# A two-layer diffusion trunk on one core: operand buffers 96 bytes further on, smaller steps between sub-layers, and one modulation unit moved

## The chip, the core and the metric

The kernel runs on one core of a Trainium2 chip. The metric is the time of one execution in microseconds on the device. The core's engines are TensorE (PE in the profile, with PEld for its weight loads), VectorE (DVE), ScalarE (ACT), GpSimd (POOL) and SyncE (SP), which here issues the loads of the weights. Each engine works through a list of instructions in order, and waits where an instruction needs the result or the buffer of another engine.

## The reference

The reference is a small model of two layers over 384 tokens of width 1024: 128 context tokens and 256 latent ones. Each layer has three sub-layers, a SwiGLU feed-forward (hidden width 2816), a token mixer (attention and convolution in layer 0, pooling and grouped-query attention in layer 1), and a second feed-forward. All is computed in 32-bit floating point. Each sub-layer normalises, scales and shifts its input, and gates its normalised output:

```python
def modulate_norm(x, g, shift, scale):
    return rms_norm(x, g) * (1.0 + scale[:, None, :]) + shift[:, None, :]

def swiglu(h, w1, w2):
    g, u = jnp.split(h @ w1, 2, axis=-1)
    return (jax.nn.silu(g) * u) @ w2
```

Shift, scale and gate come from SiLU of a conditioning vector through a linear map of its own for each layer, nine vectors of 1024 per layer and per kind of token.

## The kernel before

The tokens lie in three tiles of 128 (tile 0 is the context, tiles 1 and 2 are latent). The six sub-layers are numbered 0 to 5: feed-forward, even mixer, feed-forward, feed-forward, odd mixer, feed-forward. A product in full precision is made of three float32r products: an operand is split in a high part (a cast on ScalarE) and a low part (a subtraction on VectorE), and `mm3` (lines 436 to 438) multiplies high by high, high by low and low by high. The activations of all tiles lie in `xh` and `xl`, columns by token.

**Weights.** They come as units of 1 MB. SP loads a unit to one of four `raw` buffers. A unit is used in two halves: `prep` casts a half to `whi` on ScalarE (line 152) and subtracts on VectorE to get `wlo` (line 155), into one of three pairs of buffers. With `defer`, the subtraction is cut in two pieces of 512 columns that are issued later. A list of units, made once by `plan()`, sets the order of the loads. The linear map of the modulation is in the list too, as units called `mod`: VectorE computes each of these in four pieces (line 229, tile `junkv`), which the kernel sets between the subtractions of the weights. `MOD_PLAN` has a pair of numbers for each sub-layer: how many modulation units stand among its weights, and how many of these in its first phase (the 22 units of the gate and up weights, `w1`). The rest stand in its second phase (the 11 units of the down weights, `w2`), spread over its first seven places.

**Second phase.** `down` multiplies the hidden activations `g` by the down weights and gathers into two PSUM banks per tile, 512 columns each. Its main part is 15 halves over all three tiles; the last halves are then done tile by tile, so that a tile's sum is ready early and can be worked on beside the others' matmuls.

**Between sub-layers.** For each tile, `post_steps` squares the sums with a running total (ScalarE, line 329, tile `junk`), multiplies them by the gate (VectorE, line 353, `ptmp`), computes one over the root of the mean square in `rstd_of` (ScalarE's square root `rq`, VectorE's `rv`, `ry`, `ra`, `rz`), and adds to the residual `x` (line 365). `stat_steps` squares the new `x`, and scales it to `xn`, one half on VectorE (line 382) and one on ScalarE (line 383). TensorE transposes `xn` into two PSUM banks (line 389), and `evac_steps` applies scale and shift from the bank into `xtmp` (line 411 on VectorE for the first two of four blocks of 128 columns, line 413 on ScalarE for the other two), and splits `xtmp` into `xh` (line 422) and `xl` (line 423). For tile 2 this runs beside the next sub-layer's first matmuls: `early(0)` to `early(3)` work on tiles 0 and 1 with a half of the weights each, and the transposes of tile 2 are issued by `between` inside `early(2)`, the third half. `late()` then does tile 2's part. A feed-forward's SiLU (line 610, tile `sil`) needs another function table on ScalarE than the square root does, which is loaded at its first use.

Of the kernel before, what the change touches and what calls it, by code (L numbers as in the profile page):

```python
# [11 lines left out]
F32 = mybir.dt.float32  # L12
# [24 lines left out]
class Trunk:  # L37
    def __init__(self, ctx, tc, io):
        self.ctx, self.tc, self.nc, self.io = ctx, tc, tc.nc, io
        nc = self.nc  # L40
        pool = lambda name, bufs=1, **kw: ctx.enter_context(tc.tile_pool(name=name, bufs=bufs, **kw))
        self.cp = pool("const")
        self.sp = pool("small", 2)
        self.wp = pool("weights")
        self.pp = pool("psum", 1, space=bass.MemoryType.PSUM)
        self.dp = pool("scratch", 1, space=bass.MemoryType.DRAM)
        self.uid = 0

        const = lambda name, shape: self.cp.tile(shape, F32, tag=name, name=name)
        cc = const("cc", [P, KC, 2])  # L50
        nc.sync.dma_start(cc, io["cond"])
        self.x = const("x", [P, NT, D])
        for t in range(NT):
            src = io["x_prompt"] if t == 0 else io["x_sample"][(t - 1) * P : t * P]
            nc.sync.dma_start(self.x[:, t, :], src)
        self.nwT = const("nwT", [P, 6, KC])
        nc.gpsimd.dma_start(self.nwT, io["norm_pre"])
        self.mbT = const("mbT", [P, 6, 3, KC])
        nc.gpsimd.dma_start(self.mbT, io["mod_bT"])
        self.npT = const("npT", [P, 6, KC])  # L60
        nc.gpsimd.dma_start(self.npT, io["norm_post"])
        self.sel = const("sel", [P, 2])
        nc.gpsimd.dma_start(self.sel, io["sel"])
        self.csT = const("csT", [P, KC, 32])
        nc.vector.memset(self.csT, 0.0)
        self.cc = cc
        self.ident = const("ident", [P, P])
        make_identity(nc, self.ident)
        self.one = const("one", [P, 1])
        nc.vector.memset(self.one, 1.0)  # L70
        self.xh = self.cp.tile([P, KC, TOK], F32R, tag="xh", name="xh")
        self.xl = self.cp.tile([P, KC, TOK], F32R, tag="xl", name="xl")
        self.gates, self.shift, self.scale = {}, {}, {}
        self.gate_rows = {}
        self.cond_rows = None
# [220 lines left out]

    def rstd_of(self, ss, n=1, ss2=None):


        nc = self.nc
        tile_ = lambda tag, dt=F32: self.sp.tile([P, n], dt, tag=f"{tag}{n}", name=self.name(tag), bufs=2)
        q, v = tile_("rq"), tile_("rv")
        if ss2 is None:
            nc.vector.tensor_scalar(v, ss, EPS, None, op0=ALU.add)
            nc.scalar.activation(q, v, AF.Sqrt)
        else:
            nc.scalar.activation(q, ss, AF.Sqrt, bias=ss2)
            nc.vector.tensor_scalar(v, ss, ss2, None, op0=ALU.add)  # L310
        y = tile_("ry")
        nc.vector.reciprocal(y, q)
        a = tile_("ra")
        z = tile_("rz")
        if n == 1:
            nc.vector.scalar_tensor_tensor(a, y, y, v, op0=ALU.mult, op1=ALU.mult)
        else:
            nc.vector.tensor_tensor(a, y, y, ALU.mult)
            nc.vector.tensor_tensor(a, a, v, ALU.mult)
        nc.vector.scalar_tensor_tensor(z, a, 3.0, y, op0=ALU.subtract, op1=ALU.mult)  # L320
        return z
# [18 lines left out]
    def post_steps(self, t, acc, s):  # L340


        nc = self.nc
        cond = 0 if t == 0 else 1
        gate = self.gates[s]
        st = {}
        cols = [slice(0, 512), slice(512, 1024)]
        square, eps, sums = self.square_steps(acc)

        def gating(h):  # L350
            if h == 1:
                st["tmp"] = self.cp.tile([P, D], F32, tag="ptmp", name=self.name("ptmp"))
            nc.vector.scalar_tensor_tensor(st["tmp"][:, cols[h]], acc[h], RS, gate[:, cond, cols[h]],  # L353
                                           op0=ALU.mult, op1=ALU.mult)

        def second():
            square(1), gating(1)

        def first():
            square(0), gating(0), eps()  # L360
            st["z"] = self.rstd_of(**sums)

        def update(h):
            xs = self.x[:, t, cols[h]]
            nc.vector.scalar_tensor_tensor(xs, st["tmp"][:, cols[h]], st["z"], xs, op0=ALU.mult, op1=ALU.add)

        return second, first, update, square, gating
# [29 lines left out]
    def evac_steps(self, t, tp, s):  # L397

        nc = self.nc
        cond = 0 if t == 0 else 1  # L400
        st = {}

        def modulate(q, dve=True, act=True):
            if q not in st:
                st[q] = self.sp.tile([P, 4, P], F32, tag=f"xtmp{q}", name=self.name("xtmp"), bufs=1)
            for c in ((0, 1) if dve else ()) + ((2, 3) if act else ()):
                k = 4 * q + c
                src, scale, shift = (tp[q][:, c * P : (c + 1) * P], self.scale[s][:, cond, k : k + 1],
                                     self.shift[s][:, cond, k : k + 1])
                if c < 2:  # L410
                    nc.vector.tensor_scalar(st[q][:, c, :], src, scale, shift, op0=ALU.mult, op1=ALU.add)
                else:
                    nc.scalar.activation(st[q][:, c, :], src, AF.Identity, bias=shift, scale=scale)  # L413

        def split(q):
            return self.split(self.xh[:, 4 * q : 4 * q + 4, t * P : (t + 1) * P],
                              self.xl[:, 4 * q : 4 * q + 4, t * P : (t + 1) * P], st[q], True)

        return modulate, split

# [160 lines left out]
    def ffn(self, s, p1, p2, rest):  # L581
        tc, nc = self.tc, self.nc
# [31 lines left out]

        def mm_half(ps2, w, h, cols, between=None):
            n = cols.stop - cols.start
            for gu in range(2):
                if gu == 1 and between:
                    between()
                for kk in range(4):  # L620
                    k = 4 * h + kk
                    c0 = kk * 256 + gu * P
                    self.mm3(ps2[gu][:, :n], w[0][:, c0 : c0 + P], w[1][:, c0 : c0 + P],
                             self.xh[:, k, cols], self.xl[:, k, cols], k == 0, k == KC - 1)

        if s == 0:
            for u in range(3):
# [1 line left out]
        else:  # L629
# [11 lines left out]
            def run_ab(n, between=None):  # L641
                u, h = divmod(n, 2)
                if pab[u] is None:
                    pab[u] = [self.psum(b) for b in (6 * u, 6 * u + 1)]
                mm_half(pab[u], ws[n], h, ab, between)
                return lambda: gate_up(u, *pab[u], ab)
# [46 lines left out]
        for n, key in enumerate(units[done:]):  # L693
# [6 lines left out]
            ps2 = [self.psum(bank), self.psum(bank + 1)]  # L700
# [13 lines left out]
    def start(self, units):  # L714


        nc, io = self.nc, self.io
        with self.tc.tile_pool(name="start", bufs=1, reuse_waits="tile") as tp:
# [50 lines left out]
            ws, sums, rowsof = {}, {}, {}  # L769
# [55 lines left out]
            def evac(g, between=None):  # L825
                for j in range(2):
                    k = 2 * g + j
                    tmp = self.sp.tile([P, TOK], F32, tag=f"xtmp{j}", name=self.name("xtmp"), bufs=1)
                    nc.vector.tensor_scalar(tmp[:, 0:P], xnT[:, k, 0:P], vec[1][:, 0, k : k + 1],
                                            vec[0][:, 0, k : k + 1], op0=ALU.mult, op1=ALU.add)  # L830
                    nc.scalar.activation(tmp[:, P:TOK], xnT[:, k, P:TOK], AF.Identity,
                                         bias=vec[0][:, 1, k : k + 1], scale=vec[1][:, 1, k : k + 1])
                    if between and j == 0:
                        between()
                    self.split(self.xh[:, k, :], self.xl[:, k, :], tmp)
# [17 lines left out]
            vectors(0, 0, 1)  # L853
            keep_warm(0, WARM2)
            evac(0, parts[0][1])
            for u in (1, 2):
                parts[u] = self.prep(1, "all")
# [8 lines left out]
            products(0, 2, (0,))  # L866
            vectors(1, 0, 1)
            evac(1)
            products(0, 2, (1,))
            mods(2, 0), mods(2, 1), rows(2, 0, 1)  # L870
# [415 lines left out]


MOD_PLAN = [
    (16, 11), (8, 8), (16, 11), (20, 14), (0, 0), (4, 4),
]  # L1290


# [145 lines left out]
```

## Time and profile before

| What | Value |
|---|---|
| median of three runs | 1452.9 us (1452.47 to 1452.91) |
| profiled execution | 1453.24 us |
| its span, first to last instruction | 1451.4 us |
| TensorE busy | 98% of the span |
| VectorE, ScalarE busy | 70%, 42% |
| mean granted TensorE clock | 0.998 |

The span is 1.84 us shorter than the execution that it was taken from. Matmuls are pipelined and their ends are modelled, so a busy share of 98% means that there was nearly always a matmul under way, and not that each ran as fast as it could: how closely the starts follow one another says that. The granted clock is the share of the full 2.4 GHz that TensorE got; 0.50 is the lower of its two levels, 1.2 GHz.

### The profile page before, as it was taken

The page shows a single profiled execution, that of the slowest core. Times are in us where ns is not written, and L with a number is a line of the kernel's source. Part 1 is how long each engine was busy: PE and PEld are TensorE (multiplying, and loading weights), DVE is VectorE, ACT ScalarE, POOL GpSimd, SP SyncE. Part 2 cuts the span into 40 slices and gives each one's busy share as a digit, 9 for nine tenths or more (in the row PEclk, how much of TensorE's full clock was granted, in tenths as well). Part 3 has the DMA queues.
Part 4 walks back from the last instruction along what each step waited for, and adds up shares of the span by engine and source line. Part 5 has one row for each costly group of instructions (what it writes and reads, how often), then busy time and mean ns, then how long its engine had stood idle before and what let it go on. Part 6 is the DMA issues. An engine that isn't in the chain of part 4 may idle for free.

```text
span 1451.4 us, 19798 instructions
## 1 busy us (share of the span) xinstructions
PE 1423.3 (98%) x7747; PEld 1298.7 (89%) x7747; DVE 1022.3 (70%) x1768; ACT 613.1 (42%) x1021; POOL 29.0 (2%) x54
## 2 busy tenths in 40 slices
PE   8999999999999999999999999999999999999998
PEld 6999998879888999998889999977886799999886
DVE  5688769569997578786675888867668765555333
ACT  5533332463555533332364333313657653333232
POOL 0000000020000000000000000000100000000000
PEclk9999999999999999999999999999999999999999
DMA  9556556636544346655733566556350334444331
GB/s 373 209 215 237 204 203 234 230 129 238 191 157 156 117 175 232 232 179 198 261 117 145 207 229 232 204 192 244 109 209 30 117 117 145 150 170 175 118 114 44
DMA packets 38958, 262.58 MB, mean 181 GB/s; under 512 B 4816, under 2 KB 4976, under 8 KB 8784
## 3 DMA queue, kind: packets, MB, share of 16 engines
q1 hardware_dynamic: 35424, 243.29, 45.5%
q0 software_dynamic: 3440, 18.02, 3.3%
q8 instruction: 61, 1.00, 0.3%
q14 instruction: 33, 0.27, 0.1%
HBM read 259.01 MB, written 2.29 MB: 180 GB/s over the span
## 4 chain that ended last, share of the span: by engine, by line
PE 88%; DVE 5%; ACT 4%; issue 2%; DMA 1%; DVEq 0%; ACTq 0%; SPq 0%; POOLq 0%
PE psB L436 27%; PE psB L438 27%; PE psB L437 27%; PE psB L389 2%; DVE junkv L229 2%; PE psB L930 1%; DVE wlo L155 1%; ACT junk L329 1%; PE psB L971 1%; ACT xtmp L413 1%; DMA raw<-in_ffn_w 1%; ACT xh L422 1%; DMA csB<-crows 0%; ACT whi L152 0%; PE psB L777 0%
## 5 line engine op out<-in xcount | busy, mean ns | idle before, releaser
L436 PE MATMUL psB<-xh,whi 128*128 128x384 f32 (+1 forms) x1536 | 518.8, 338 | 0.7 <-ACT qz L1073 0.4
L438 PE MATMUL psB<-xh,wlo 128*128 128x384 f32 (+1 forms) x1536 | 514.0, 335 | 1.8 <-DVE wlo L155 1.8
L437 PE MATMUL psB<-xl,whi 128*128 128x384 f32 (+1 forms) x1536 | 514.3, 335 | 0.5 <-DVE xl L423 0.3
L155 DVE TENSOR_TENSOR wlo<-raw,whi 128x1024 fp32r<-128x1024 f32 (+2 forms) x286 | 336.2, 1185 | 130.4 <-ACT whi L152 128.7
L152 ACT CAST whi<-raw 128x1024 fp32r<-128x1024 f32 (+1 forms) x275 | 285.5, 1044 | 320.1 <-PE psB L437 146.9
L229 DVE CUSTOM_DVE_ANT_0 junkv<-raw,csB,mbT 128x1024 bf16<-128x1024 f32 x256 | 327.9, 1281 | 8.2 <-DMA csB<-crows 3.4
L436 PEld LDWEIGHTS psB<-xh,whi 128*128 128x128 f32 x1536 | 288.1, 188 | 5.6 <-issue 2.3
L437 PEld LDWEIGHTS psB<-xl,whi 128*128 128x128 f32 x1536 | 288.1, 188 | 3.0 <-DVE xl L423 2.0
L438 PEld LDWEIGHTS psB<-xh,wlo 128*128 128x128 f32 x1536 | 288.0, 188 | 2.8 <-DVE wlo L155 2.4
L436 PE MATMUL psB<-whi,g 128*128 128x512 f32 x384 | 150.9, 393 | 2.7 <-ACT whi L152 2.7
L437 PE MATMUL psB<-wlo,g 128*128 128x512 f32 x384 | 150.4, 392 | 2.3 <-DVE wlo L155 2.3
L438 PE MATMUL psB<-whi,g 128*128 128x512 f32 x384 | 150.2, 391 | 0.0
L422 ACT CAST g<-gt 128x384 fp32r<-128x384 f32 (+1 forms) x84 | 42.5, 506 | 191.3 <-DVE gt L612 191.3
L612 DVE TENSOR_TENSOR gt<-psB,sil 128x384 f32<-128x384 f32 (+1 forms) x88 | 48.1, 547 | 95.4 <-PE psB L438 87.6
L436 PEld LDWEIGHTS psB<-whi,g 128*128 128x128 f32 x384 | 72.5, 189 | 19.0 <-ACT whi L152 3.9
L437 PEld LDWEIGHTS psB<-wlo,g 128*128 128x128 f32 x384 | 72.5, 189 | 18.0 <-DVE wlo L155 3.2
L438 PEld LDWEIGHTS psB<-whi,g 128*128 128x128 f32 x384 | 72.4, 189 | 15.1
L610 ACT ACTIVATE sil<-psB 128x384 f32<-128x384 f32 (+1 forms) x88 | 42.7, 485 | 91.2 <-PE psB L438 91.1
L423 DVE TENSOR_TENSOR g<-gt,g 128x384 fp32r<-128x384 f32 (+1 forms) x84 | 46.1, 549 | 48.1 <-ACT g L422 48.1
L353 DVE SCALAR_TENSOR_TENSOR ptmp<-psB,gate 128x512 f32<-128x512 f32 x36 | 24.8, 690 | 39.1 <-ACT junk L329 38.7
L436 PE MATMUL psB<-g,g 128*128 128x512 f32 x120 | 47.0, 392 | 0.0
L436 PE MATMUL psB<-whi,xh 128*128 128x512 f32 (+1 forms) x120 | 42.4, 353 | 4.5 <-ACT xh L422 2.2
(227 smaller groups left out, 1433.7 us busy)
## 6 DMA issues: line engine op xcount, KB each, us to landing
raw<-in_ffn_w SPq DMA_DIRECT2D x129, 1024.0 KB, 4.9
raw<-in_mod_w SPq DMA_DIRECT2D x64, 1024.0 KB, 4.8
raw<-in_ev_in SPq DMA_DIRECT2D x10, 1024.0 KB, 7.3
m<-in_mod_first SPq DMA_DIRECT2D x8, 1024.0 KB, 12.7
gate<-gscr POOLq DMA_DIRECT2D x6, 1024.0 KB, 4.9
csB<-crows POOLq DMA_DIRECT2D x4, 1024.0 KB, 6.9
raw<-in_ev_out SPq DMA_DIRECT2D x4, 1024.0 KB, 4.9
raw<-in_od_out SPq DMA_DIRECT2D x4, 1024.0 KB, 4.9
```

What stands on the lines that cost most here:

```text
L152: nc.scalar.copy(hi, src)
L155: sub = lambda hi=hi[:, c], lo=lo[:, c], src=src[:, c]: nc.vector.tensor_tensor(lo, src, hi.bitcast(F32), ALU.subtract)
L229: nc.vector.tensor_tensor_reduce(junk, self.raw[i][0][:, kk * D : (kk + 1) * D], self.csB[:, c, :], 1.0, self.mbT[:, s, kind, k : k + 1], ...
L353: nc.vector.scalar_tensor_tensor(st["tmp"][:, cols[h]], acc[h], RS, gate[:, cond, cols[h]], op0=ALU.mult, op1=ALU.mult)
L389: self.nc.tensor.transpose(out, src, self.ident)
L422: self.nc.scalar.copy(hi, src)
L423: sub = lambda: self.nc.vector.tensor_tensor(lo, src, hi.bitcast(F32), ALU.subtract)
L436: nc.tensor.matmul(out, ah, bh, start=first, stop=False)
L437: nc.tensor.matmul(out, ah, bl, start=False, stop=False)
L438: nc.tensor.matmul(out, al, bh, start=False, stop=last)
L610: nc.scalar.activation(sil[:, :n], pg[:, :n], AF.Silu)
L612: nc.vector.tensor_tensor(gt[:, :n], pu[:, :n], sil[:, :n], ALU.mult)
```

## The change

The change has five parts.

1. A constant `one`, which took 4 bytes in each partition, takes 100. All tiles that are allocated after it move by 96 bytes: `xh`, `xl`, `junk`, `xn`, `ptmp`, `gate`, `raw`, `whi`, `wlo`, `g` and smaller ones. Before, `raw`, `whi`, `wlo` and `g` lay at multiples of 128 bytes, and `xh` at 64 past a multiple of 128. Their distances from each other stay.
2. In `first()`, the step after the first half's squares, `rstd_of` issues the square root and `rv` ahead of the gating of the first half, and the reciprocal behind it.
3. `evac_steps` has a tile `xtmp` for each engine and bank, 2 x 128 columns, where one tile of 4 x 128 was written by both engines. So the split has four casts and four subtractions of 256 columns for a tile of tokens, where it had two of each with 512.
4. In `mm_half` with `between`, the third half's matmuls run over blocks 0 and 1 of the gate part, then blocks 0 and 1 of the up part, then the transposes, then blocks 2 and 3 of both. Before, all four blocks of the gate part stood ahead of the transposes, and the up part behind them. Twelve matmuls stand ahead of them in both.
5. `MOD_PLAN` moves one modulation unit from sub-layer 3 to sub-layer 2, from the second phase of the one to the first phase of the other.

A sixth edit takes the temporary tile of the first evacuation of the kernel from another pool, since the old tags are gone.

```diff
-        self.one = const("one", [P, 1])
+        self.one = const("one", [P, 25])[:, 0:1]
...
             nc.vector.tensor_scalar(v, ss, ss2, None, op0=ALU.add)
+        if between:
+            between()
         y = tile_("ry")
...
         def first():
-            square(0), gating(0), eps()
-            st["z"] = self.rstd_of(**sums)
+            eps(), square(0)
+            st["z"] = self.rstd_of(**sums, between=lambda: gating(0))
...
         def modulate(q, dve=True, act=True):
-            if q not in st:
-                st[q] = self.sp.tile([P, 4, P], F32, tag=f"xtmp{q}", name=self.name("xtmp"), bufs=1)
-            for c in ((0, 1) if dve else ()) + ((2, 3) if act else ()):
...
+            for e in ((0,) if dve else ()) + ((1,) if act else ()):
+                st[q, e] = self.sp.tile([P, 2, P], F32, tag=f"xtmp{q}{e}", name=self.name("xtmp"), bufs=1)
+                for j in range(2):
...
         def split(q):
-            return self.split(self.xh[:, 4 * q : 4 * q + 4, t * P : (t + 1) * P],
-                              self.xl[:, 4 * q : 4 * q + 4, t * P : (t + 1) * P], st[q], True)
+            subs = []
+            for e in range(2):
+                k = 4 * q + 2 * e
+                subs.append(self.split(self.xh[:, k : k + 2, t * P : (t + 1) * P],
+                                       self.xl[:, k : k + 2, t * P : (t + 1) * P], st[q, e], True))
+            return lambda: [f() for f in subs]
...
         def mm_half(ps2, w, h, cols, between=None):
             n = cols.stop - cols.start
-            for gu in range(2):
-                if gu == 1 and between:
+            order = [(gu, kk) for kks in (((0, 1), (2, 3)) if between else ((0, 1, 2, 3),)) for gu in range(2)
+                     for kk in kks]
+            for i, (gu, kk) in enumerate(order):
+                if i == 4 and between:
                     between()
...
 MOD_PLAN = [
-    (16, 11), (8, 8), (16, 11), (20, 14), (0, 0), (4, 4),
+    (16, 11), (8, 8), (17, 12), (19, 14), (0, 0), (4, 4),
 ]
```

The moved unit changes the order in which SP issues the loads. In sub-layer 3's second phase (`in_ffn_w` are units of the down weights here, `in_mod_w` of the modulation), ten rows of SP's list read like this before:

```order
L119 DMA raw_8572<-in_ffn_w 128x2048
L119 DMA raw_8574<-in_mod_w 128x2048
L119 DMA raw_8644<-in_ffn_w 128x2048
L119 DMA raw_8668<-in_mod_w 128x2048
L119 DMA raw_8700<-in_ffn_w 128x2048
L119 DMA raw_8724<-in_mod_w 128x2048
L119 DMA raw_8757<-in_ffn_w 128x2048
L119 DMA raw_8781<-in_mod_w 128x2048
L119 DMA raw_8813<-in_ffn_w 128x2048
L119 DMA raw_8837<-in_ffn_w 128x2048
```

and like this after, at the same ten places:

```order
L119 DMA raw_8566<-in_mod_w 128x2048
L119 DMA raw_8636<-in_ffn_w 128x2048
L119 DMA raw_8638<-in_mod_w 128x2048
L119 DMA raw_8708<-in_ffn_w 128x2048
L119 DMA raw_8732<-in_ffn_w 128x2048
L119 DMA raw_8765<-in_mod_w 128x2048
L119 DMA raw_8789<-in_ffn_w 128x2048
L119 DMA raw_8821<-in_mod_w 128x2048
L119 DMA raw_8867<-in_ffn_w 128x2048
L119 DMA raw_8877<-in_ffn_w 128x2048
```

Before, modulation and weight units alternate until the last modulation unit. After, two weight units stand next to each other at the fourth and fifth of these places. The last modulation unit stands at the eighth place in both.

On TensorE, the third half of sub-layer 3's first units stands around the transposes of tile 2 (`psB_1334` is the bank of the gate part, `psB_1335` that of the up part). Before:

```order
L436 MATMUL psB_1334_6950<-xh,whi_6877 128x256
L437 MATMUL psB_1334_6950<-xl,whi_6877 128x256
L438 MATMUL psB_1334_6950<-xh,wlo_6878 128x256
L389 MATMUL psB_1336_6964<-ident,xn_6898 128x128 x4
L389 MATMUL psB_1337_6965<-ident,xn_6898 128x128 x4
L436 MATMUL psB_1335_6951<-xh,whi_6877 128x256
L437 MATMUL psB_1335_6951<-xl,whi_6877 128x256
L438 MATMUL psB_1335_6951<-xh,wlo_6878 128x256
L436 MATMUL psB_1335_6951<-xh,whi_6877 128x256
```

and after (banks `psB_1356` and `psB_1357` are the gate and the up part):

```order
L443 MATMUL psB_1357_7010<-xh,whi_6936 128x256
L444 MATMUL psB_1357_7010<-xl,whi_6936 128x256
L445 MATMUL psB_1357_7010<-xh,wlo_6937 128x256
L391 MATMUL psB_1358_7023<-ident,xn_6957 128x128 x4
L391 MATMUL psB_1359_7024<-ident,xn_6957 128x128 x4
L443 MATMUL psB_1356_7009<-xh,whi_6936 128x256
L444 MATMUL psB_1356_7009<-xl,whi_6936 128x256
L445 MATMUL psB_1356_7009<-xh,wlo_6937 128x256
L443 MATMUL psB_1356_7009<-xh,whi_6936 128x256
```

Ahead of the transposes stand now blocks 0 and 1 of the up part where blocks 2 and 3 of the gate part stood, and the gate part's blocks 2 and 3 come behind.

On VectorE, the same boundary has, from the subtractions of tile 1 to the step behind the reciprocal, before:

```order
L423 TENSOR_TENSOR xl<-xtmp_6845,xh 128x4x128
L423 TENSOR_TENSOR xl<-xtmp_6850,xh 128x4x128
L353 SCALAR_TENSOR_TENSOR ptmp_6855<-psB_1183_6157,gate_5279 128x512
L335 TENSOR_SCALAR ss_1270_6641<-ss_1270_6641 128x1
L310 TENSOR_SCALAR rv_6868<-ss_1270_6641 128x1
L312 RECIPROCAL ry_6871<-rq_6867 128x1
L316 SCALAR_TENSOR_TENSOR ra_6873<-ry_6871,rv_6868 128x1
L320 SCALAR_TENSOR_TENSOR rz_6874<-ra_6873,ry_6871 128x1
```

and after:

```order
L430 TENSOR_TENSOR xl<-xtmp_6898,xh 128x2x128
L430 TENSOR_TENSOR xl<-xtmp_6901,xh 128x2x128
L430 TENSOR_TENSOR xl<-xtmp_6904,xh 128x2x128
L430 TENSOR_TENSOR xl<-xtmp_6907,xh 128x2x128
L337 TENSOR_SCALAR ss_1288_6688<-ss_1288_6688 128x1
L310 TENSOR_SCALAR rv_6926<-ss_1288_6688 128x1
L355 SCALAR_TENSOR_TENSOR ptmp_6910<-psB_1200_6204,gate_5315 128x512
L314 RECIPROCAL ry_6930<-rq_6925 128x1
L318 SCALAR_TENSOR_TENSOR ra_6932<-ry_6930,rv_6926 128x1
L322 SCALAR_TENSOR_TENSOR rz_6933<-ra_6932,ry_6930 128x1
```

The subtractions are four instead of two, the small steps on `ss` and `rv` have moved ahead of the gating that writes `ptmp`, and the reciprocal stands right behind it. ScalarE's list changes with it: the casts to `xh` are four where they were two.

## Rows read from the trace of the kernel before

**Rows 1.** the page: busy time by engine, and the chain that ended last.

```profile
PE 1423.3 (98%) x7747; PEld 1298.7 (89%) x7747; DVE 1022.3 (70%) x1768; ACT 613.1 (42%) x1021; POOL 29.0 (2%) x54
...
PE 88%; DVE 5%; ACT 4%; issue 2%; DMA 1%; DVEq 0%; ACTq 0%; SPq 0%; POOLq 0%
```

**Rows 2.** waits of TensorE, whole span: total us, times, longest us.

```profile
PE psB L436 <- ACT xh L422: 2.4, 5, 0.6
PE psB L438 <- DVE wlo L155: 1.8, 3, 0.6
PE psB L436 <- ACT sil L610: 1.2, 3, 0.4
PE psB L436 <- DVE ss L335: 1.0, 1, 1.0
...
PE psB L438 <- DVE xl L423: 0.7, 3, 0.2
...
PE psB L437 <- DVE xl L423: 0.3, 2, 0.2
```

**Rows 3.** windows: us, busy us by engine, granted clock, DMA share, GB/s.

```profile
663.30:724.50 61.20, 61.20 (x272) 50.56 (x272) 46.30 (x62) 17.82 (x18) 0.50 (x1) 1.00 0.64 237
945.70:1015.00 69.30, 64.35 (x271) 51.45 (x270) 51.03 (x68) 17.77 (x18) 0.00 (x0) 0.98 0.58 215
973.10:976.50 3.40, 3.40 (x9) 2.64 (x8) 3.36 (x6) 0.00 (x0) 0.00 (x0) 0.50 0.00 0
```

**Rows 4.** timeline of SP: load issues in sub-layer 3's main part of down.

```profile
953.41 0.33 SPq L119 DMA_DIRECT2D raw<-in_ffn_w  x1
...
964.37 0.33 SPq L119 DMA_DIRECT2D raw<-in_ffn_w  x1
```

**Rows 5.** timeline of ScalarE at the same place.

```profile
958.36 2.00 ACT L152 CAST whi<-raw 128x1024 fp32r<-128x1024 f32 x2 [7.18 <-DMA raw<-in_ffn_w]
```

**Rows 6.** timeline of VectorE at the same place.

```profile
963.12 1.22 DVE L155 TENSOR_TENSOR wlo<-raw,whi 128x1024 fp32r<-128x1024 f32 x1
```

**Rows 7.** timeline of TensorE, from sub-layer 2 to 3, tile 2.

```profile
763.37 1.04 PE L389 MATMUL psB<-ident,xn 128*128 128x128 f32 x8
...
766.34 0.39 PE L436 MATMUL psB<-whi,xh 128*128 128x256 f32 x1 [0.52 <-ACT xh L422]
...
770.35 0.38 PE L436 MATMUL psB<-whi,xh 128*128 128x256 f32 x1 [0.41 <-ACT sil L610]
```

**Rows 8.** timeline of ScalarE, same stretch.

```profile
754.05 1.15 ACT L422 CAST xh<-xtmp 128x512 fp32r<-128x512 f32 x2
...
757.39 0.29 ACT L309 ACTIVATE rq<-ss 128x1 f32<-128x1 f32 x1 [0.88 <-DVE ss L335]
...
761.64 0.72 ACT L383 ACTIVATE xn<-x,rz 128x512 f32<-128x512 f32 x1 [0.68 <-DVE rz L320]
764.83 0.81 ACT L413 ACTIVATE xtmp<-psB,mv,mv 128x128 f32<-128x128 f32 x2 [2.47 <-DVE xtmp L411]
...
768.62 1.28 ACT L610 ACT_TABLE_LOAD   x1
```

**Rows 9.** timeline of VectorE, same stretch.

```profile
756.54 0.69 DVE L353 SCALAR_TENSOR_TENSOR ptmp<-psB,gate 128x512 f32<-128x512 f32 x1 [0.53 <-ACT junk L329]
...
757.72 0.16 DVE L312 RECIPROCAL ry<-rq 128x1 f32<-128x1 f32 x1 [0.17 <-ACT rq L309]
...
764.01 1.37 DVE L411 TENSOR_SCALAR xtmp<-psB,mv,mv 128x128 f32<-128x128 f32 x4 [1.28 <-PE psB L389]
```

**Rows 10.** groups of ScalarE by shape: count, busy us, mean ns.

```profile
L422 ACT CAST g<-gt 128x256 fp32r<-128x256 f32 x6 | 2.4, 406 | 2.9 <-DVE gt L612 2.9
```

**Rows 11.** windows that hold 384-column matmuls.

```profile
112.00:212.00 100.00, 100.00 (x579) 99.91 (x578) 76.11 (x105) 36.14 (x48) 1.05 (x2) 1.00 0.60 217
777.00:917.00 140.00, 140.00 (x795) 139.97 (x794) 114.49 (x163) 49.68 (x67) 0.00 (x0) 1.00 0.59 209
```

**Rows 12.** groups of TensorE by shape (L437 and L438 count the same).

```profile
L436 PE MATMUL psB<-xh,whi 128*128 128x384 f32 x1464 | 498.5, 341 | 0.7 <-ACT qz L1073 0.4 <-ACT xh L422 0.2
```

More of the change, by code (lines that the diff above doesn't have):

```diff
@@ L295, in mod_vec, with rstd_of @@
         return self.sp.tile([P, 2, KC], F32, tag=("shift", "scale", "gatev")[kind], name=self.name("mv"))
-    def rstd_of(self, ss, n=1, ss2=None):
+    def rstd_of(self, ss, n=1, ss2=None, between=None):
         nc = self.nc
@@ L403, in modulate @@
         def modulate(q, dve=True, act=True):
-            if q not in st:
-                st[q] = self.sp.tile([P, 4, P], F32, tag=f"xtmp{q}", name=self.name("xtmp"), bufs=1)
-            for c in ((0, 1) if dve else ()) + ((2, 3) if act else ()):
[L407 to L413, printed above, removed]
-        def split(q):
-            return self.split(self.xh[:, 4 * q : 4 * q + 4, t * P : (t + 1) * P],
-                              self.xl[:, 4 * q : 4 * q + 4, t * P : (t + 1) * P], st[q], True)
+            for e in ((0,) if dve else ()) + ((1,) if act else ()):
+                st[q, e] = self.sp.tile([P, 2, P], F32, tag=f"xtmp{q}{e}", name=self.name("xtmp"), bufs=1)
+                for j in range(2):
+                    c = 2 * e + j
+                    k = 4 * q + c
+                    src, scale, shift = (tp[q][:, c * P : (c + 1) * P], self.scale[s][:, cond, k : k + 1],
+                                         self.shift[s][:, cond, k : k + 1])
+                    if e == 0:
+                        nc.vector.tensor_scalar(st[q, e][:, j, :], src, scale, shift, op0=ALU.mult, op1=ALU.add)
+                    else:
+                        nc.scalar.activation(st[q, e][:, j, :], src, AF.Identity, bias=shift, scale=scale)
+        def split(q):
+            subs = []
[4 more added lines that the diff above has]
+            return lambda: [f() for f in subs]
         return modulate, split
@@ L616, in mm_half @@
             n = cols.stop - cols.start
-            for gu in range(2):
-                if gu == 1 and between:
+            order = [(gu, kk) for kks in (((0, 1), (2, 3)) if between else ((0, 1, 2, 3),)) for gu in range(2)
+                     for kk in kks]
+            for i, (gu, kk) in enumerate(order):
+                if i == 4 and between:
                     between()
[L620 to L624, printed above, removed]
+                k = 4 * h + kk
+                c0 = kk * 256 + gu * P
+                self.mm3(ps2[gu][:, :n], w[0][:, c0 : c0 + P], w[1][:, c0 : c0 + P],
+                         self.xh[:, k, cols], self.xl[:, k, cols], k == 0, k == KC - 1)
         if s == 0:
@@ L827, in evac @@
                     k = 2 * g + j
-                    tmp = self.sp.tile([P, TOK], F32, tag=f"xtmp{j}", name=self.name("xtmp"), bufs=1)
+                    tmp = self.cp.tile([P, D], F32, tag=("xn", "ptmp")[j], name=self.name("xtmp"))[:, :TOK]
                     nc.vector.tensor_scalar(tmp[:, 0:P], xnT[:, k, 0:P], vec[1][:, 0, k : k + 1],
```

## The prediction

> **What bounds the kernel now.** I read the page first: TensorE is busy for 98% of the span, and the chain of work that ended last runs through it for 88%, with 5% on VectorE and 4% on ScalarE [rows 1]. So an edit can only give time where TensorE stands still, or where its matmuls follow each other more slowly. The list of what TensorE waited for, over the whole span, says where it stands: 2.4 us in five waits for ScalarE's `xh`, 1.8 us in three waits for VectorE's `wlo`, 0.7 us in three for `xl`, 0.3 us in two for an earlier `xl` (line 437), 1.2 us in three for ScalarE's `sil`, and 1.0 us once for VectorE's `ss` [rows 2]. Those are small. The larger loss is seen by laying the same stage of two sub-layers side by side: the main part of `down` takes 61.20 us in sub-layer 2 with 272 matmuls, and 69.30 us in sub-layer 3 with 271, of which 3.40 us were run at a granted clock of 0.50, the lower of TensorE's two levels (1.2 GHz) [rows 3]. That is 8.1 us in one place.
>
> **The moved unit.** In sub-layer 3 the weight loads of this stage leave one at a time: SP issues one at 953.41 and the next at 964.37 us [rows 4]. ScalarE's two casts of the first one start at 958.36, after 7.18 us of idling for that load [rows 5], and VectorE's last subtraction of it starts at 963.12 and takes 1.22, so it ends at 964.34, 0.03 us before the next issue [rows 6]. So each load waits until the buffer of the unit just before it is free, and a unit costs 964.37 - 953.41 = 10.96 us. TensorE uses one unit in 36 matmuls (two halves, three tiles, two banks, three products), which at 61.20 / 272 = 0.225 us is 8.1 us. The other three of the four `raw` buffers hold modulation units in that stage, since the listing of loads alternates strictly there. After the change two weight loads stand in a row within this run, as they do in the same stage of sub-layer 2 before the change, and from there on the weight loads find two buffers instead of one. I take sub-layer 2 as the price: 69.30 - 61.20 = 8.1 us less. The moved unit itself adds four modulation pieces to sub-layer 2's first phase, which then has 12 units where sub-layer 3 carries 14 in the same number of weight units; I cost it at nothing. What hides it is VectorE's free time beside 8 us of matmuls per unit; if that cover failed, a stall like the present one would appear there (a rival below). Bounds: 0 and 8.1.
>
> **The evacuations.** I follow tile 2 from sub-layer 2 to 3. Before, TensorE stops for the second `wlo` piece (one of those three waits), transposes at 763.37, gets the first `xh` at 766.34, and stands again for `sil` until 770.35 [rows 7]. Call the transposes' start T.
>
> Ahead of T there are two limits. The first is TensorE's own stalls: the split third half needs only the first `wlo` piece ahead of T, which saves the 0.6 us of that wait (1.8 us in three [rows 2]) and about 0.15 us for the slow matmul behind it, and halving the casts of tile 1 lets the first `xl` come before TensorE asks for it: 0.3 us in two waits [rows 2], so 0.15, and as much again for the slow matmul after the restart, 0.3. Together 1.1 in round figures. The second is when `xn` is ready. VectorE's `ptmp` starts at 756.54 and takes 0.69, and the reciprocal comes at 757.72 [rows 9]; the `sqrt` (`rq`) idled 0.88 us for VectorE's `ss` [rows 8]. Now `sqrt` and `rv` go ahead of `ptmp`, so the reciprocal follows 0.2 + 0.6 us after the squares end instead of 1.2: -0.4. Against it, the two casts of 1.15 us [rows 8] become four of 406 ns each [rows 10] at a spacing of some 0.33, 1.37 in all: +0.2. So `xn`, whose ScalarE half ends at 761.64 + 0.72 = 762.36 [rows 8], comes at about 762.2. Both limits give T = 762.25, a gain of 1.1 us.
>
> Behind T, the casts of VectorE's part need no wait on ScalarE and are half as long: first `xh` at T + 2.67 instead of 766.34 - 763.37 = T + 2.97. TensorE would gain 0.6 us up to the last `xl`. But it then meets the wait for `sil`: ScalarE must still do both modulations, four short casts, a whole `whi` cast and the 1.28 us table load at 768.62 [rows 8], and the four casts cost what the two did. `sil` comes at T + 7.0 as before (770.35 - 763.37 = 6.98), so the 0.6 us moves into that wait. Three boundaries into a feed-forward sub-layer (1 to 2, 2 to 3, 4 to 5) have this form: 3 x 1.1 = 3.3 us. At 0 to 1 the mixer has no `sil`; there the 0.6 behind T counts, and 0.2 ahead of it: 0.8. At 3 to 4 TensorE waits for VectorE's `ss` step, that is for the last reading of its bank [rows 2]; `ptmp` now comes 0.2 later behind `rv` and 0.2 later behind the casts, which about eats the 0.4 that `xh` and `xl` give: 0. After the last matmul of the kernel the same reordering saves 0.4. Sum of the evacuations: 4.5 us. Bounds: 2.0, if `xn` keeps its old time plus 0.2 (three times 0.7 and nothing else); and 6.5, if the waits for `xh`, `wlo` and `xl` all go (2.4 + 1.8 + 0.7, with 0.1 for each of some twelve restarts and the 0.4 at the end).
>
> ScalarE's modulation starts at 764.83 after 2.47 us of idling that VectorE's `xtmp` ends [rows 8]; VectorE itself starts at 764.01 [rows 9]. With a tile for each engine it might seem that this wait goes, which would bring ScalarE's chain and `sil` forward by the difference, 0.8 us, at each of those three boundaries, 2.5 in all. In the built program the wait stands as before, on VectorE's step on that PSUM bank, so I count nothing. The Trainium skill ("PSUM — Partial Sum Buffer", section on bank collisions) says that two engines must be kept apart on one bank by a semaphore, reads included. By that rule the wait stays and the gain is 0, as I have it; without it the sum would be 2.5 us larger.
>
> **The pad.** It moves `xh`, `xl`, `raw`, `whi`, `wlo` and `g` by 96 bytes. Nothing in the trace reads these tiles at such addresses, so I bound it. What can change is how fast matmuls follow: 384-column matmuls ran 579 in 100.00 us in one stretch (0.1727 us each) and 795 in 140.00 in another (0.1761) on the same addresses [rows 11], so the spacing has steps of some 3.4 ns for reasons that are not the address alone. There are 3 x 1464 of them [rows 12], and one step on all of these is 15 us; on all 7747 matmuls of the page [rows 1] it is 26 us. A part runs at the fast spacing already, so the most that can be won is less than 15: I put it at 10. Between -10 and +26 I take 0: neither direction has a row that is nearer, and the spacing moved within one set of addresses. For the loads, the Trainium skill ("DMA: Bandwidth & Descriptors", section on how a descriptor splits into AXI transactions) has a descriptor that starts off a 256-byte boundary take one more transaction; for 8 KB rows that is an estimate of 33 for 32, or the 4.95 us from issue to cast (958.36 - 953.41, [rows 4, 5]) becoming 5.1, which no run here shows and which the sum does not hold.
>
> The sum is 8.1 + 4.5 + 0 = 12.6 us off the profiled execution's 1453.24, or 1440.6; the median of the runs, 1452.9, lies 0.3 lower, so 1440.
>
> **Rivals.**
> A. The load stall stays or moves: the loads of sub-layer 3 still go one at a time, or sub-layer 2, with a unit more and a gate row among its pieces, takes over the stall. For it: the margin is one buffer. Against it: the same layout runs at 61.20 us in sub-layer 2. Then 1453 - 4.5 = 1448.
> B. The pad costs one step of the matmul spacing. This alone ends slower: 26 us of loss on 7747 matmuls against 12.6 of gain, 1466; it decides once the step is above 12.6 us / 7747 = 1.6 ns. For it: the spacing has such steps [rows 11]. Against it: the steps seen came without a move of addresses, so addresses need not be what sets them.
> C. The pad helps by up to 10 us: 1430 to 1436.
> D. The evacuation gains are given back, at `sil` or at the first gates: 1444 to 1445.
>
> **How the numbers follow.** 0.2% is 2.9 us, about what a measurement of this kernel can tell from no change: faster means below 1450.0, slower above 1455.8. Forecast 0.50 (its own range 1436 to 1443), C 0.15, A 0.15, D 0.08, B 0.12. Faster: all of the forecast, C and D, 0.11 of A, 0.84 in all. Slower: 0.10 of B. Same: the rest, 0.06. For 8 in 10 I leave out B, the upper edge of A and the lower edge of C: 1429 to 1450.
>
> **What would show it.** Sub-layer 3's main part of `down` at 61 us and a granted clock of 1.00 throughout; no wait of TensorE for `wlo` ahead of tile 2's transposes; the reciprocal directly behind `ptmp`; the wait for `sil` grown from 0.4 to some 1.0 us in each of three places; matmuls of 384 columns between 0.1727 and 0.1761 us. The prediction is wrong if that spacing leaves this band, or if weight loads in sub-layer 2 or 3 lie 11 us apart.

## The result and the profile after

The changed kernel takes 1438.26 us in the median of four executions, against 1452.91 for the kernel before in the same session: 14.65 us less. One of the four ran at two thirds of the clock from end to end (2001.94 us) and counts in that median, and in nothing else here. The other three took 1432.51, 1437.02 and 1439.5 us, so the middle one of them is 15.9 us faster than the kernel before. Their ratio to the kernel before is 0.9887, with a 95% interval of 0.9856 to 0.9917, which is 16.4 us less. The profiled execution took 1439.5 us and has a span of 1437.6. One thing differs from before at once: the executions of the kernel before lie 0.6 us apart in that session (and 4 us over all sessions, 1451.17 to 1455.14), and these three 7 us.

What TensorE waited for, over the whole span of the changed kernel (total us, times, longest us), answers to [rows 2]:

```profile
PE psB L443 <- ACT sil L617: 2.8, 3, 1.0
PE psB L443 <- ACT qz L1081: 2.0, 1, 2.0
PE psB L443 <- DVE ry L314: 1.0, 1, 1.0
PE psB L443 <- ACT xh L429: 0.9, 5, 0.2
...
PE psB L444 <- DVE wlo L155: 0.5, 1, 0.5
...
PE psB L444 <- DVE xl L430: 0.2, 1, 0.2
```
The waits for `xh`, `wlo` and `xl` have shrunk or gone: the 1.8 us for `wlo` ahead of the transposes is no more in the list, and `xh` is 0.9 us where it was 2.4. The wait for `sil` has grown from 1.2 to 2.8 us in the same three places. And there is a new one, 2.0 us for `qz`, which the prediction did not have.

Two waits stand above those of [rows 2] in the list of the kernel before:

```profile
PE psB L437 <- DVE wlo L155: 3.8, 5, 1.2
PE psB L436 <- ACT whi L152: 2.7, 3, 1.4
```
All of the 2.7 us, and 2.3 of the 3.8, lie in sub-layer 3's second phase: this is where TensorE stood still for the late weight loads. Both of these are gone; the 0.5 us for `wlo` that are left lie at the boundary from sub-layer 0 to 1.

The windows of sub-layer 3's main part of `down`, and of a stretch in the first mixer behind the new wait:

```profile
943.30:1004.60 61.30, 61.30 (x272) 50.77 (x271) 45.96 (x61) 17.91 (x19) 0.00 (x0) 1.00 0.66 245
335.00:338.00 3.00, 3.00 (x11) 3.00 (x10) 2.96 (x6) 0.48 (x1) 0.00 (x0) 0.50 0.84 292
```
The first answers to [rows 3]: 61.30 us with 272 matmuls and the full clock, where 69.30 us were needed. (Of the 8 us, 5.0 are the two waits above, and some 1.7 are lost in the 3.40 us at half the clock.) In the second the granted clock is 0.50, the lower level: TensorE, after standing still for `qz`, ran at 1.2 GHz for a while.

SP's load issues at the same place, as in [rows 4]:

```profile
941.07 0.33 SPq L119 DMA_DIRECT2D raw<-in_ffn_w  x1
...
952.06 2.86 SPq L119 DMA_DIRECT2D raw<-in_ffn_w  x2
962.90 0.33 SPq L119 DMA_DIRECT2D raw<-in_mod_w  x1
965.43 0.33 SPq L119 DMA_DIRECT2D raw<-in_ffn_w  x1
```
Two weight loads leave close together (the row that starts at 952.06 holds both), and the next one is not held up behind a unit that has just been split. From 941.07 to 952.06 there are still 10.99 us between two weight loads, but TensorE waits for none of them in this stage.

The timeline of TensorE at the boundary from sub-layer 2 to 3 in the changed kernel, as in [rows 7]:

```profile
761.32 1.03 PE L391 MATMUL psB<-ident,xn 128*128 128x128 f32 x8
...
763.93 0.39 PE L443 MATMUL psB<-whi,xh 128*128 128x256 f32 x1 [0.17 <-ACT xh L429]
...
768.19 0.39 PE L443 MATMUL psB<-whi,xh 128*128 128x256 f32 x1 [0.93 <-ACT sil L617]
```

ScalarE at the same boundary, as in [rows 8]:

```profile
752.74 1.33 ACT L429 CAST xh<-xtmp 128x256 fp32r<-128x256 f32 x4
...
755.41 0.29 ACT L309 ACTIVATE rq<-ss 128x1 f32<-128x1 f32 x1
...
760.06 0.72 ACT L385 ACTIVATE xn<-x,rz 128x512 f32<-128x512 f32 x1 [0.68 <-DVE rz L322]
...
762.78 0.81 ACT L416 ACTIVATE xtmp<-psB,mv,mv 128x128 f32<-128x128 f32 x2 [1.99 <-DVE xtmp L414]
...
766.46 1.28 ACT L617 ACT_TABLE_LOAD   x1
767.75 0.38 ACT L617 ACTIVATE sil<-psB 128x256 f32<-128x256 f32 x1
```

And VectorE, as in [rows 9]:

```profile
755.41 0.21 DVE L310 TENSOR_SCALAR rv<-ss 128x1 f32<-128x1 f32 x1 [0.57 <-ACT junk L331]
755.54 0.68 DVE L355 SCALAR_TENSOR_TENSOR ptmp<-psB,gate 128x512 f32<-128x512 f32 x1
756.14 0.15 DVE L314 RECIPROCAL ry<-rq 128x1 f32<-128x1 f32 x1
```
Four casts take 1.33 us where two took 1.15. `rv` and `rq` start together, `ptmp` follows, and the reciprocal comes 0.73 us behind `rv`. The first `xh` comes 2.61 us after the transposes' start (it was 2.97), and the restart behind `sil` 6.87 us after it (it was 6.98), with 0.93 us of waiting.

### The profile page after: what moved, and what is told of

It reads as the page before. It is cut to its first block, busy times and chain, and to the rows that moved or that the text cites. A ratio compares the mean times of both kernels' runs of the same rounds, so it can differ in the third digit from the quotient of the medians.

```text
span 1437.6 us, 19880 instructions
## 1 busy us (share of the span) xinstructions
PE 1417.9 (99%) x7747; PEld 1299.1 (90%) x7747; DVE 1021.9 (71%) x1798; ACT 614.6 (43%) x1051; POOL 29.0 (2%) x54
## 4 chain that ended last, share of the span: by engine, by line
PE 93%; ACT 3%; DVE 3%; DMA 1%; issue 1%; DVEq 0%; SPq 0%; ACTq 0%
PE psB L443 29%; PE psB L444 29%; PE psB L445 29%; PE psB L391 2%; PE psB L938 1%; PE psB L979 1%; ACT xtmp L416 1%; DMA csB<-crows 1%; ACT junk L331 1%; ACT xh L429 1%; PE psB L785 0%; DVE xtmp L414 0%; ACT whi L152 0%; DVE wlo L155 0%; ACT L617 0%
## 5 line engine op out<-in xcount | busy, mean ns | idle before, releaser
L443 PE MATMUL psB<-g,g 128*128 128x512 f32 x120 | 47.0, 391 | 0.0
L445 PE MATMUL psB<-g,g 128*128 128x512 f32 x120 | 46.8, 390 | 0.0
L444 PE MATMUL psB<-g,g 128*128 128x512 f32 x120 | 46.7, 389 | 0.0
```

Of the source, the lines that this page charges most:

```text
L443: nc.tensor.matmul(out, ah, bh, start=first, stop=False)
L444: nc.tensor.matmul(out, ah, bl, start=False, stop=False)
L445: nc.tensor.matmul(out, al, bh, start=False, stop=last)
```

## Experiments

**The moved unit alone.**

```diff
-    (16, 11), (8, 8), (16, 11), (20, 14), (0, 0), (4, 4),
+    (16, 11), (8, 8), (17, 12), (19, 14), (0, 0), (4, 4),
```

> The kernel before with the moved modulation unit alone. My theory: the weight loads of sub-layer 3's second phase stop going one at a time, its main part of down takes 61.2 us instead of 69.3, and the time is 1453 - 8.3 = 1444.6 us. Rival (the stall moves to sub-layer 2): 1449 to 1453, with weight loads 11 us apart in sub-layer 2.

Measured: 1445.34 us against 1453.27 (ratio 0.9946, 0.9935 to 0.9958), 7.9 us less, and 0.3 us between executions. The window of sub-layer 3's main part:

```profile
945.40:1006.70 61.30, 61.30 (x272) 50.79 (x271) 45.95 (x60) 17.80 (x18) 0.00 (x0) 1.00 0.65 244
```
It is 8 us shorter than in [rows 3], and sub-layer 2 has taken over no stall: TensorE has no wait for `whi` left anywhere. Rival A falls.

**The edits between sub-layers alone**: parts 2, 3 and 4 of the change, with the sixth edit; no pad, no moved unit.

```diff
+            eps(), square(0)
+            st["z"] = self.rstd_of(**sums, between=lambda: gating(0))
...
+                st[q, e] = self.sp.tile([P, 2, P], F32, tag=f"xtmp{q}{e}", name=self.name("xtmp"), bufs=1)
...
+            order = [(gu, kk) for kks in (((0, 1), (2, 3)) if between else ((0, 1, 2, 3),)) for gu in range(2)
+                     for kk in kks]
```

> The kernel before with the three edits between sub-layers (square root ahead of the gating, a tile for each engine, the third half split), no pad and no moved unit. My theory: 1.4 us at each of the three boundaries into a feed-forward sub-layer, some 1 us around the odd mixer, 0.5 at the end, less up to 1 us that the first mixer gives back: 1453 - 5 = 1448 us. Rival (the gains are given back at sil and at the first mixer): 1451 to 1453.

Measured: 1447.04 us (0.9959, 0.9947 to 0.9971), 6.2 us less. With the 7.9 of the run before that makes 14.1.

**The pad alone, and the change without it.**

```diff
-        self.one = const("one", [P, 1])
+        self.one = const("one", [P, 25])[:, 0:1]
```

> The kernel before with the 96-byte pad alone. My theory: the pad does nothing, 1452.9 us, and runs agree within 0.5 us as before. Rival P (the pad changes how closely matmuls follow, in some runs more than in others): 1446 to 1453, with a spread of several us between runs, as the changed kernel has (1432.5 to 1439.5).

> The changed kernel without the pad. My theory: the same as with it, 1438 us, and the same spread of some 7 us between runs, since the spread comes from a transfer into csB that lands late in the first mixer in some runs. Rival P (the pad carries a part of the gain and the spread): 1439.5 us in all runs, within 0.5.

Measured: the pad alone gives 1450.99 us in the median of 12 executions (0.998, 0.9969 to 0.9991), which is 2.3 us less, but these lie anywhere from 1445.84 to 1455.11. The change without the pad takes 1438.94 us (0.9903, 0.989 to 0.9915), from 1437.78 to 1440.01. So the wide spread comes with the pad, and my theory that a late transfer makes it falls. Rival P of the expectation is the nearer one, though its 0.5 us without the pad were too narrow (2.2 measured). The clock is not the cause either: it is 0.998 or 0.999 in all 12 executions of the pad alone.

**Which operands.** The weights and `g` moved by 96 bytes and the activations left, and the activations moved by 96 with the weights moved by 128:

```diff
+        nc.vector.memset(self.wp.tile([P, 24], F32, tag="wpad", name="wpad"), 1.0)
```

```diff
-        self.one = const("one", [P, 1])
+        self.one = const("one", [P, 25])[:, 0:1]
...
+        nc.vector.memset(self.wp.tile([P, 8], F32, tag="wpad", name="wpad"), 1.0)
```

> The kernel before with raw, whi, wlo, g and what lies behind them moved by 96 bytes, and xh, xl and the tiles of the evacuations left where they were. The pad alone spread the time over 1445.8 to 1455.1 us. Theory W (the spread comes from the weights and g, as TensorE reads them or as the loads write them): the same spread of some 9 us here. Theory A (it comes from xh and xl): runs agree within 2.5 us around 1453.

> The kernel before with xh, xl and the tiles of the evacuations moved by 96 bytes, and raw, whi, wlo and g moved by 128. Theory A: the spread of some 9 us here. Theory W: runs agree within 2.5 us around 1453.

So in the second of these two kernels both operands move, by different amounts.

Measured: the weights alone make the kernel slower, 1459.35 us (1.0041, 1.0029 to 1.0053), with 3 us between executions; the activations alone make it faster, 1447.39 us (0.9963, 0.9951 to 0.9975), with executions from 1444.6 to 1452.63. One profile of each shows a part of how. Two windows that hold only 384-column matmuls (the counts take in those that a window cuts at its ends), first in the kernel before:

```profile
505.00:555.00 50.00, 50.00 (x285) 50.00 (x284) 37.23 (x52) 17.15 (x23) 0.00 (x0) 1.00 0.48 174
570.00:650.00 80.00, 80.00 (x460) 80.00 (x459) 63.08 (x89) 28.57 (x38) 0.00 (x0) 1.00 0.60 222
```

The same windows with the weights moved:

```profile
505.00:555.00 50.00, 50.00 (x285) 50.00 (x284) 35.26 (x48) 17.58 (x23) 0.00 (x0) 1.00 0.48 171
570.00:650.00 80.00, 80.00 (x455) 80.00 (x454) 63.24 (x89) 28.57 (x38) 0.55 (x1) 1.00 0.58 210
```

And with the activations moved:

```profile
505.00:555.00 50.00, 50.00 (x285) 50.00 (x284) 37.04 (x52) 17.50 (x24) 0.00 (x0) 1.00 0.49 170
570.00:650.00 80.00, 80.00 (x464) 80.00 (x463) 65.00 (x91) 29.62 (x39) 0.00 (x0) 1.00 0.58 214
```
In the same 80 us TensorE starts 460, 455 and 464 matmuls. From start to start these are 0.1747, 0.1767 and 0.1733 us in the mean over the whole stretch, steps of 1.4 and 2.0 ns. The three kernels have the same lists. The other kernels without moved addresses have different lists and, in these two windows, the spacing of the kernel before. So where the operands lie bears on the spacing. It is not the distance between them alone: the pad alone leaves that distance as it was, and spreads the times.

The spacing is not the whole difference. With the weights moved, 4.1 of the profile's 5.8 us lie in the long stretches of such matmuls, and 0.9 in sub-layer 3's second phase, where the clock falls twice instead of once. With the activations moved, the long stretches are 2.5 us shorter and that phase is 1.3 us longer; this profile is of the slowest execution (1452.63 us), so what makes the fastest ones 8 us shorter is not in it. Of the two theories neither holds alone: the wide spread came in the run with the activations moved, and the weights alone shift the level.

**The changed kernel once more.**

> The changed kernel once more, for its spread. If the pad spreads it as it spreads the kernel before: 1432 to 1441 us. If the spread is csB landing late in the first mixer: at most 4 us between runs, and the profile shows TensorE's wait for qz growing and shrinking with the time.

Measured: 1435.36 us (0.9876, 0.9862 to 0.989; 1434.34 to 1437.05), and this profile caught a change of spacing. The same two windows:

```profile
505.00:555.00 50.00, 50.00 (x291) 50.00 (x290) 38.10 (x54) 18.06 (x24) 0.00 (x0) 1.00 0.51 190
570.00:650.00 80.00, 80.00 (x464) 80.00 (x463) 69.56 (x100) 29.18 (x39) 0.00 (x0) 1.00 0.62 224
```
The first holds 291 matmuls, where the other profile of the same kernel has 285 in that window, as the kernel before has: 0.1733 us each against 0.1767, over a stretch of 358 matmuls, which is 1.2 us. The second has 464 for 460, another 0.8. One program, two spacings. The two other long stretches (742 matmuls each) stood at 0.1767 in both profiles; if they change too, they are worth 2.5 us each, which makes 7.0 in all, as much as lies between the executions. That the fastest executions are such cases is only argued, since no profile caught all of them. The wait for `qz` was 2.0 us in the one profile and 1.5 in the other, too little for the spread.

**The parts between sub-layers, one at a time**, one execution each: part 2, part 3, and part 4 of the change alone.

```diff
-            square(0), gating(0), eps()
+            eps(), square(0)
```

> The kernel before with the square root and rv ahead of the gating alone. My theory: xn and the second wlo piece behind it come 0.4 us earlier, so the transposes of tile 2 come 0.4 us earlier at the four boundaries where TensorE waits for that wlo piece, and the end 0.4: span 1451.4 - 2.0 = 1449.4 us. Rival (ahead of the transposes only TensorE's own order counts): 1451.

```diff
-            for c in ((0, 1) if dve else ()) + ((2, 3) if act else ()):
+            for e in ((0,) if dve else ()) + ((1,) if act else ()):
```

> The kernel before with a tile for each engine and the casts of 256 columns alone. My theory: four casts are 0.2 us longer than two, which puts xn and the transposes 0.2 us later at each boundary; behind the transposes xh and xl come 0.6 us earlier, which the wait for sil eats at three boundaries and which counts at the first mixer: span 1451.4 within 0.5. Rival (shorter casts are a gain by themselves): 1.4 us at three boundaries, 1447.

```diff
-            for gu in range(2):
-                if gu == 1 and between:
+            for i, (gu, kk) in enumerate(order):
+                if i == 4 and between:
```

> The kernel before with the third half split around the transposes alone. My theory: the wait for the second wlo piece ahead of the transposes goes, and the transposes come 0.8 us earlier, where xn bounds them, at the three boundaries into a feed-forward sub-layer; nothing changes behind them: span 1451.4 - 2.3 = 1449.1 us. Rival (the wait only moves behind the transposes): 1451.

Measured, by span and by when tile 2's transposes start after tile 1's at the three boundaries into a feed-forward sub-layer:

| Kernel | span, us | the three transposes, us |
|---|---|---|
| before | 1451.4 | |
| part 2, square root ahead | 1447.4 | -0.9, -0.9, -0.8 |
| part 3, tiles and casts | 1451.3 | +0.1, +0.1, +0.2 |
| part 4, third half split | 1447.4 | -0.9, -0.8, -0.8 |
| the whole change | 1437.6 | -1.2, -1.2, -1.2 |

Part 4 gives what was expected at the transposes, but not because `xn` bounds them: TensorE has no gap ahead of them. (Of its 4.0 us, 1.1 is not its own: the last long stretch ran at 0.1747 us per matmul in that execution, where the kernel before has 0.1767.) Part 3 is worth nothing alone, as expected. Part 2 gives twice what I had. Its VectorE rows:

```profile
754.63 0.68 DVE L355 SCALAR_TENSOR_TENSOR ptmp<-psB,gate 128x512 f32<-128x512 f32 x1
755.23 0.15 DVE L314 RECIPROCAL ry<-rq 128x1 f32<-128x1 f32 x1
```
`ptmp` to reciprocal is 0.60 us, where [rows 9] have 1.18: that is the step I had. The rest lies ahead of it: the squares of tile 2 also start 0.45 us earlier after tile 1's transposes. I read this as the same edit at work for tile 1, where it frees VectorE sooner for the steps that ScalarE waits for; it wasn't tried apart. Parts 2 and 4 don't add up: 0.9 and 0.8 give 1.2 together, since both work on the same moment, the start of the transposes.

**Loading SiLU's table early.** The change without the pad, and behind `xn` of tile 2:

```diff
             xn2 = scale()
+            if s in (1, 2, 4):
+                warm = self.cp.tile([P, 512], BF16, tag="junk", name=self.name("junk"))
+                nc.scalar.activation(warm[:, 0:1], self.one, AF.Silu)
```

> The changed kernel without the pad, and with a SiLU of a single column on ScalarE right behind its half of xn of tile 2, so that the function table is loaded while ScalarE waits for the transposes. My theory (the gain behind the transposes was eaten by the wait for sil, which hangs on the 1.28 us table load): 1.1 us less at three boundaries, 1438.9 - 3.3 = 1435.6 us. Rival (the next wait, for a weight half or for the gated product, stands right behind it): 1438 to 1439.

Measured: 1435.95 us (0.9882, 0.987 to 0.9895), 3.0 us less than the change without the pad, where 3.3 were expected. ScalarE at the boundary from 2 to 3:

```profile
759.38 1.28 ACT L561 ACT_TABLE_LOAD   x1
...
761.33 0.81 ACT L416 ACTIVATE xtmp<-psB,mv,mv 128x128 f32<-128x128 f32 x2 [0.45 <-DVE xtmp L414]
...
764.88 0.39 ACT L620 ACTIVATE sil<-psB 128x256 f32<-128x256 f32 x1
```
The 1.28 us table load lies in time in which ScalarE waited for the transposes anyway, its modulation waits 0.45 us instead of 1.99, and `sil` follows the `whi` cast directly, with no table load between. The wait for `sil` is gone from TensorE's list.

**Together.** The change with the early SiLU, and the weights moved by 128 bytes:

> The changed kernel with the early SiLU, and with the weights and g moved by 128 bytes where xh, xl and the evacuations' tiles stay moved by 96. If spacing hangs on where xh and xl lie beside the weights, as the run with xh and xl moved alone showed (5.5 us less in the median, 8 us of spread), this gives 1435.9 - 5.5 = 1430 us with the same spread. Rival (that gain was chance between executions): 1435 to 1436.

Measured: 1434.18 us (0.9869, 0.9852 to 0.9885), with 0.8 us between executions. That is the lowest median of all, 1.8 us below the run without the moved addresses, but not the 1430 that I expected; the rival's 1435 is nearer. In its profile the long stretches are 2.6 us shorter than without the moved addresses, as much as in the run with the activations moved: the first half of sub-layer 0's (0.1767) and the one at 0.1747 went to 0.1733, and most of the rest stayed at 0.1767. The four executions lie 0.8 us apart although `xh` and `xl` lie where they lay in the run with 8 us of spread. So their place alone does not make the spread. Against the changed kernel's second set (1435.36) the intervals overlap.

## Why the prediction was right, point by point

The forecast of 1440 us was 1.7 us above the measured median, and the range held it. It is 3.0 us above the middle one of the three other executions, and that is the fairer distance; the 1.7 owe something to luck. The terms say the same: 8.1 + 4.5 + 0 were forecast, and 7.9 + 6.2 + 2.3 = 16.4 measured one by one.

**The moved unit: right.** 8.1 us forecast; 7.9 measured alone, and 8.3 us less in the traces from the first steps of sub-layer 3 to its end. The step that carries it is the reading of [rows 4 to 6], one free buffer for weight loads in sub-layer 3. The program bears it out: the five weight loads that alternate with modulation units in the list before go to one and the same of the four buffers, and those in the list after to all four. Two things were read too simply. The waits that belong to the stall, 2.7 and 2.3 us, are not among those that the prediction took from the list. And the sign of being wrong, weight loads 11 us apart, is met by its letter in the changed kernel (10.99 us, ahead of the two that leave together) with nothing lost; what counts is whether TensorE waits behind.

**The evacuations: the mechanism right, the size low.** 4.5 us forecast, 6.2 measured alone. Three terms were off. At the boundaries I had 1.1 each; it is 1.2 at the transposes and 0.2 behind them, 1.4 in all, or 4.3 us for the three instead of 3.3. Of the two limits ahead of the transposes, TensorE's own stalls were sized right. The other, `xn`, was not: its ScalarE half ends at 760.78 in the changed kernel, 0.7 us earlier after tile 1's transposes than before, where I had 0.15, and 0.54 us ahead of the transposes' start. So it bounds nothing there, and that both limits gave the same T in the sum was an accident of the sizes. It bounds nothing with part 4 or part 2 alone either, where the transposes follow the matmul ahead of them without a gap. At 3 to 4 I set the later `ptmp` against the earlier `xh` and came to 0; the wait for that bank did not change (1.0 us in both lists), the other waits there shrank, and it is 1.0 to 1.3 us less in the kernels with all parts. At 0 to 1 the transposes came 0.7 us earlier where I had 0.2, but behind them, where I had a gain of 0.6, the mixer gave back 0.4 to 1.2 us.

**What gave it back** is the new wait for `qz`. In the changed kernel VectorE stands in front of a modulation piece until `csB` has arrived, and TensorE then waits for `qz` behind it:

```profile
327.16 1.28 DVE L229 CUSTOM_DVE_ANT_0 junkv<-raw,csB,mbT 128x1024 bf16<-128x1024 f32 x1 [4.96 <-DMA csB<-crows]
```

TensorE's row behind it:

```profile
333.76 0.45 PE L443 MATMUL psB<-xh,whi 128*128 128x384 f32 x1 [2.00 <-ACT qz L1081]
```
The kernels with part 3 show it, the one with part 2 alone does not. VectorE's row with part 3 alone:

```profile
327.39 1.28 DVE L229 CUSTOM_DVE_ANT_0 junkv<-raw,csB,mbT 128x1024 bf16<-128x1024 f32 x1 [4.33 <-DMA csB<-crows]
```

And with part 2 alone:

```profile
326.18 1.28 DVE L229 CUSTOM_DVE_ANT_0 junkv<-raw,csB,mbT 128x1024 bf16<-128x1024 f32 x1 [3.41 <-DMA csB<-crows]
```
`csB` took 8.1 to 8.7 us to land in all kernels with part 3, and 7.0 to 7.2 in those without. In the former it is issued 0.2 us ahead of a load of the modulation weights instead of 0.3 behind it, and a weight load follows after some 3.0 us instead of 3.5. That the three transfers share the queues more closely is what I take for the cause; no run set it apart. TensorE's wait for `qz`, 0.2 to 0.4 us in the kernels without part 3, is 1.4 to 2.0 in those with it. In the changed kernel's first profile the low clock behind it cost 1.5 us more on the spot, but against the change without the pad, which waited 2.0 us too and kept the full clock, only 0.3 us of that are left at the mixer's end. This is rival D in a small form: not at `sil`, but in the mixer behind.

**The wait for `sil`: right.** It grew from 0.4 to 0.9 us each, and the run with the early table load shows that the load was what TensorE waited for.

**The modulation's wait on the PSUM bank** stands as forecast: 1.99 us, ended by VectorE's `xtmp`, though the two engines now write tiles of their own. The Trainium skill ("PSUM — Partial Sum Buffer", section on bank collisions) and the trace agree here.

**The pad: the value 0 was wrong, the bounds held.** Alone it is worth 2.3 us in the median, and between executions from 7 less to 2 more. I reasoned that the spacing changes without a move of addresses, so that addresses need not set it. The runs show both: the level changes with addresses (0.1767 throughout with the weights moved, 0.1733 in more stretches with the activations moved), and on some addresses it is not the same in every execution. Moving the weights alone goes the way of rival B (6.4 us slower), and moving the activations, with the weights by 128 bytes, the way of C (5.5 us faster); the two do not add up to the pad. The changed kernel's second set, 1435.36 us, lies in C's range.

The band of 0.1727 to 0.1761 us was counted in windows that take in the matmuls cut at their ends. From start to start the same stretches of the kernel before have 0.1733 and 0.1767, and the changed kernel stays within these. The bound of 26 us was too wide, since it held 512-column matmuls, which kept 0.227 us in every run.

For the loads, the median from issue to landing of the 1 MB weight loads is 4.9 us with `raw` moved and without. The extra transaction that the Trainium skill ("DMA: Bandwidth & Descriptors", section on how a descriptor splits into AXI transactions) has for such an address is not to be seen in it.

## What to carry to other kernels

Lay the same stage of different layers side by side: the one that takes 8 us longer with the same matmuls shows the defect and its price at once, here a run of loads in which all buffers but one are held by another stream. Edits ahead of a join don't add up, so cost them together; and look at the next wait behind, since a gain is kept only up to it (here a table load, which one tiny instruction moved into idle time). When a kernel nearly always has a matmul under way, measure the spacing from start to start by stretch before and after any move of buffers, and over several executions.

## What was not expected of the hardware

The spacing of float32r matmuls of 384 columns took three values in the long stretches of these runs, 0.1733, 0.1747 and 0.1767 us from start to start, each constant over hundreds of matmuls. It changed with the place of the operands in SBUF at the same order of instructions (460, 455 or 464 starts in the same 80 us), and in one program it differed between two executions (285 and 291 starts in 50 us). It changed too without any moved address: once in a long stretch, in the run of part 4 alone (0.1747 where 0.1767 stood), and in the short one of 144 matmuls in the first mixer (0.1747 in the kernel before, 0.1767 with the moved unit alone). What decides it in an execution stays open. The matmuls of 512 columns showed none of it, with 0.227 us in every run.
